# A decoder layer's last mixer projection, computed with seven block products in place of eight

## The chip, the core and the metric

The kernel runs on one core of one Trainium2 chip. A core has five engines that run side by side, each through its own list of instructions in order: PE multiplies matrices, DVE, ACT and POOL work on vectors, SP issues transfers. Engines wait for each other through semaphores. The metric is the time of one execution in microseconds (us) on the device, the median over the runs; lower is better. The profiler's trace is one execution of its own.

## The reference

One layer, 512 tokens of 1024 features, float32: a SwiGLU, a token mixer with two branches, a second SwiGLU, each added to the residual, and a final norm.

```python
x = x + 0.5 * swiglu(rms_norm(x, ffn1_norm), ffn1_w_gate, ffn1_w_up, ffn1_w_down)
x = x + token_mixer(rms_norm(x, mix_norm), w_in, ..., w_o)
x = x + 0.5 * swiglu(rms_norm(x, ffn2_norm), ffn2_w_gate, ffn2_w_up, ffn2_w_down)
return rms_norm(x, final_norm)
...
def swiglu(x, w_gate, w_up, w_down):
    return (jax.nn.silu(x @ w_gate) * (x @ w_up)) @ w_down
...
merged = jax.nn.sigmoid(g_a) * y_a + jax.nn.sigmoid(g_b) * y_b
return merged @ w_o                       # the end of token_mixer
```

The change is about the last line: `merged` is 512 x 1024, `w_o` is 1024 x 1024.

## The kernel before

**Matrix products.** Every float32 operand is split into a high part, rounded to the type that PE multiplies fast (fp32r), and the low rest; a product is three matmuls, high by high, high by low, low by high. A weight arrives by a transfer on SP's queue into `raw` (128 x 1024, 512 KB), ACT casts it to `whi`, DVE subtracts to `wlo`. There are four buffers of each of the three, and `stream` lists all pieces of weights in the order of their use; `weights()` (line 626) takes the next and has the following ones made.

**Stages.** First SwiGLU (`ffn_up_raw`, then `ffn_down`), the mixer's input projections and its recurrence (steps in the order of the table `MIXER`), the products of the two branches (the last is `ps_ob`, from line 1345), the output projection `rows` (771), the second SwiGLU (`ffn_up`, `ffn_down`).

**The output projection.** `m` holds eight tiles of `merged`, transposed: 128 features by 512 tokens. `rows` takes the eight pieces of `w_o`, and for each of four groups of 128 tokens and each half of 512 output features adds three matmuls of 512 columns to one of eight PSUM banks `ps_o`: 8 x 4 x 2 x 3 = 192 matmuls. The last three pieces (`TAIL`, 56) are run group by group, so that the groups end one after the other. Behind each group `mixed` (1373) adds the bank to the residual `x` (numbered tiles in the traces: one for each group and half), stores it to `x2d` and calls `renorm` (755): sums of squares on ACT (`sq`), root on ACT (after a load of its function table), reciprocal on DVE, scaled rows `xn` on DVE, four transposes on PE for each half into `ps_xt`, and from there on ACT and DVE the split operand `xh`, `xl` of the second SwiGLU, or the differences of tokens that it wants (`xt`, `t`, `tf1h` and so on, from `token_sums`, 813).

**Seven products for eight.** `ffn_up` and `ffn_down` cut both operands into 2 x 2 blocks and use the scheme that needs seven block products and some sums of blocks. The sums of the weights are made in DRAM, by transfers that copy and add (`transfer`, 519), issued on POOL's own DMA queue; the sums of the other operand (`form`) on DVE, split by `half_parts` (689): a cast on ACT and a subtraction on POOL, or for `VG` on whichever of DVE and POOL the planner takes. The products of `ffn_down` (922) go to pairs of banks `ps_dx`, `ps_dv`, `ps_dw`, in the order `DOWN_ORDER = (0, 2, 5, 4, 6, 3, 7)` (74), and `onto` adds each to the rows of the residual it belongs to. Product 3 ends token groups 0 and 1, product 7 groups 2 and 3, and `done` is called there. `ffn_up` starts with the products that read groups 0 and 1 alone (`UP_ORDER`, 72).

**Order.** `step_sums` (575) records the next transfer of the list `queue` at certain steps. All instructions are recorded first; `Plan.order` (251) then puts each engine's list in order, by program order among those whose operands are ready on its own estimate of durations. The engines follow these lists as they stand.

Of the kernel before, what the change touches and what calls it, by code (L numbers as in the profile page):

```python
# [55 lines left out]
TAIL = 3  # L56
# [393 lines left out]
def layer_kernel(ctx: ExitStack, tc: tile.TileContext, xT, x, vecs, cst, gu1, dn1, win, wout, wo, gu2, dn2, lora, gateup, gmix, gff2, gfin, out):  # L450
# [94 lines left out]
    def down_sums(name, w):  # L545
        got, groups = {}, []
        for j0 in range(0, FJ, 4):
            groups.append([])
            n = min(4, FJ - j0)
# [14 lines left out]
    def down_stream(w, downs):  # L564
        for b in DOWN_ORDER:
            for j in range(0, FJ, 2):
                n = min(2, FJ - j) * S
# [30 lines left out]
    for kt in range(KT):  # L598
        stream.append((wo[kt], D))
# [171 lines left out]
    def rows(hs, done):  # L771

        n = len(hs)
        accs = [[psum("ps_o") for _ in range(2)] for _ in range(NQ)]

        def one_row(ft, q, w, halves):
            hhi, hlo = hs[ft]
            whi, wlo = w
            for lh, r, k in ((hhi, whi, 0), (hhi, wlo, 1), (hlo, whi, 2)):
                for hf in halves:  # L780
                    T.matmul(accs[q][hf], lhsT=lh[:, sl(q)], rhs=r[:, hf * S:(hf + 1) * S],
                             start=ft == 0 and k == 0, stop=ft == n - 1 and k == 2)

        for ft in range(n - TAIL):
            w = weights()
            for q in range(NQ):
                one_row(ft, q, w, (0, 1))
            step_sums()
        tail = [weights(0) for ft in range(n - TAIL, n)]
        for q in range(NQ):  # L790
            for hf in range(2):
                for i in range(TAIL):
                    one_row(n - TAIL + i, q, tail[i], (hf,))
            done(q, accs[q])

# [126 lines left out]
    def ffn_down(hs, parts, res, done):  # L922

        banks = {n: [psum(n) for _ in range(2)] for n in ("ps_dx", "ps_dv", "ps_dw")}
# [23 lines left out]
        def onto(q, hf, ps, sign):  # L948
            x = res[q][hf]
            V.scalar_tensor_tensor(out=x, in0=ps, scalar=0.5 * sign, in1=x, op0=ALU.mult, op1=ALU.add)  # L950
# [3 lines left out]
        for b in DOWN_ORDER:  # L954
            ps = banks[{2: "ps_dv", 4: "ps_dw", 3: "ps_dw"}.get(b, "ps_dx")]
            x = forms.get(b) or [None] * FJ

            def one(j, w, rs):
# [387 lines left out]
    for dt in range(KT):  # L1346
# [63 lines left out]
def _layout(np, inp):  # L1410
# [27 lines left out]
    o["wo"] = w["w_o"].reshape(KT, P, D)  # L1438
# [32 lines left out]
```

## Time and profile before

| | us |
|---|---|
| median of the three runs | 1145.55 |
| lowest and highest of them | 1141.31, 1150.65 |
| the profiled execution | 1142.87 |
| its span, first to last instruction | 1141.1 |

In the profile a row of the timeline has the start (us from the span's start), the duration, engine, line, operation, tiles, shapes and count; in brackets stands the idle time of the engine ahead of it and what ended it. Nearly all rows have line 437, a helper that records every operation, so tiles tell the place. The table of stretches gives the busy time of each engine with the number of instructions in parentheses, the granted TensorE clock (1.00 is full), the share of the sixteen DMA engines' time and the rate.

### The profile page before, as it was taken

Reading aid. Unit: us, or ns where it says so; the run is one execution under the profiler, and the core shown is the slowest. Engines: PE = TensorE matmul, PEld = TensorE weight load, DVE = VectorE, ACT = ScalarE, POOL = GpSimd, SP = SyncE. Lnnn points to the kernel's source line nnn. Section 1 sums busy time; section 2 is a strip of 40 time slices with the busy share of each in tenths; the row PEclk is TensorE's granted clock in tenths of the full one; section 3 lists DMA queues with packets and bytes.
Section 4 is the critical chain, followed back from the end, with each engine's and each line's share of the span. In section 5 each row is a group of like instructions: output and inputs, shape, how many; then the busy total and the mean of one; then the engine's idle time right before and its main releaser. Section 6 shows DMA issues by size and latency. Waiting matters only on the chain.

```text
span 1141.1 us, 17088 instructions
## 1 busy us (share of the span) xinstructions
PE 1110.3 (97%) x6572; PEld 945.6 (83%) x6572; DVE 761.2 (67%) x1041; ACT 559.7 (49%) x964; POOL 305.3 (27%) x336
## 2 busy tenths in 40 slices
PE   8999999999999899989999999999999999999997
PEld 6888888888887777878777788888999999998886
DVE  5754454468867589995758742363987766768875
ACT  6422332236735776343655642333665555556744
POOL 4122121136840154234311121100011111217840
PEclk9999999999999989989999999999999999999999
DMA  8568686678899189889156679953576688875563
GB/s 307 171 221 222 239 219 197 177 189 278 282 296 362 43 193 280 232 237 256 53 139 180 154 226 330 306 179 116 174 221 248 213 216 271 229 246 185 190 190 119
DMA packets 67202, 244.87 MB, mean 215 GB/s; under 512 B 7089, under 2 KB 8113, under 8 KB 62129
## 3 DMA queue, kind: packets, MB, share of 16 engines
q1 hardware_dynamic: 48816, 151.51, 38.5%
q0 software_dynamic: 18304, 92.28, 32.4%
q8 instruction: 51, 0.84, 0.3%
q14 instruction: 31, 0.25, 0.1%
HBM read 237.47 MB, written 98.57 MB: 294 GB/s over the span
## 4 chain that ended last, share of the span: by engine, by line
PE 78%; DVE 8%; issue 6%; DMA 3%; ACT 2%; POOL 2%; SPq 0%; ACTq 0%; POOLq 0%; DVEq 0%
PE ps_gu L437 20%; PE ps_in L437 12%; PE ps_wx L437 11%; PE ps_dx L437 8%; PE ps_ww L437 5%; PE ps_o L437 4%; PE ps_dw L437 4%; PE ps_wc L437 3%; PE ps_dv L437 3%; PE ps_ob L437 2%; DVE wlo L437 2%; PE ps_oa L437 2%; DMA raw<-in_dn_dram 1%; DVE tmp L437 1%; PE ps_f L437 1%
## 5 line engine op out<-in xcount | busy, mean ns | idle before, releaser
L437 ACT CAST whi<-raw 128x1024 fp32r<-128x1024 f32 (+2 forms) x273 | 271.8, 997 | 441.8 <-issue 103.5
L437 DVE TENSOR_TENSOR wlo<-raw,whi 128x1024 fp32r<-128x1024 f32 (+2 forms) x273 | 333.6, 1228 | 184.1 <-ACT whi L437 178.5
L437 POOL TENSOR_TENSOR hp<-gg,hp 128x256 fp32r<-128x256 f32 x117 | 133.3, 1170 | 439.6 <-ACT hp L437 439.6
L437 PE MATMUL ps_gu<-xh,whi 128*128 128x512 f32 x352 | 137.1, 392 | 3.3 <-ACT whi L437 3.3
L437 PE MATMUL ps_in<-xl,whi 128*128 128x512 f32 (+1 forms) x360 | 137.5, 383 | 0.0
L437 PE MATMUL ps_in<-xh,wlo 128*128 128x512 f32 (+1 forms) x360 | 137.3, 382 | 0.0
L437 PE MATMUL ps_gu<-xl,whi 128*128 128x512 f32 x352 | 137.2, 391 | 0.0
L437 PE MATMUL ps_gu<-xh,wlo 128*128 128x512 f32 x352 | 137.2, 391 | 0.0
L437 PE MATMUL ps_in<-xh,whi 128*128 128x512 f32 (+1 forms) x360 | 137.0, 381 | 0.0
L437 PE MATMUL ps_dx<-whi,hp 128*128 128x512 f32 x352 | 112.8, 397 | 0.0
L437 PEld LDWEIGHTS ps_gu<-xh,whi 128*128 128x128 f32 x352 | 66.3, 188 | 18.6 <-ACT whi L437 4.6
L437 PEld LDWEIGHTS ps_dx<-whi,hp 128*128 128x128 f32 x352 | 66.6, 189 | 15.4
L437 PEld LDWEIGHTS ps_in<-xh,whi 128*128 128x128 f32 x360 | 68.2, 190 | 13.0 <-issue 0.4
L437 PEld LDWEIGHTS ps_in<-xl,whi 128*128 128x128 f32 x360 | 68.3, 190 | 12.6
L437 PEld LDWEIGHTS ps_in<-xh,wlo 128*128 128x128 f32 x360 | 68.2, 190 | 12.3
L437 PEld LDWEIGHTS ps_gu<-xh,wlo 128*128 128x128 f32 x352 | 66.6, 189 | 13.9
L437 PEld LDWEIGHTS ps_gu<-xl,whi 128*128 128x128 f32 x352 | 66.4, 189 | 13.8
L437 PE MATMUL ps_dx<-wlo,hp 128*128 128x512 f32 x176 | 69.8, 397 | 0.0
L437 DVE TENSOR_TENSOR uu<-ps_gu,rstd 128x512 f32<-128x512 f32 x22 | 15.2, 690 | 62.9 <-PE ps_gu L437 62.9
L437 PE MATMUL ps_dw<-whi,hp 128*128 128x512 f32 x176 | 55.6, 393 | 0.0
L437 ACT CAST hp<-gg 128x256 fp32r<-128x256 f32 x132 | 48.7, 404 | 13.1 <-DVE gg L437 13.0
L437 POOL DMA_DIRECT2D us<-in_gu_dram x36 | 30.7, 855 | 71.7 <-issue 60.4
(307 smaller groups left out, 2378.0 us busy)
## 6 DMA issues: line engine op xcount, KB each, us to landing
raw<-in_gu_dram SPq DMA_DIRECT2D x75, 512.0 KB, 4.1
us<-in_gu_dram POOLq DMA_DIRECT2D x30, 1024.0 KB, 9.5
raw<-us SPq DMA_DIRECT2D x44, 512.0 KB, 4.9
raw<-in_win_dram SPq DMA_DIRECT2D x42, 512.0 KB, 6.0
raw<-in_dn_dram SPq DMA_DIRECT2D x30, 512.0 KB, 4.7
d1s<-in_dn_dram POOLq DMA_DIRECT2D x12, 1024.0 KB, 8.3
ds<-in_dn_dram POOLq DMA_DIRECT2D x12, 1024.0 KB, 21.3
raw<-d1s SPq DMA_DIRECT2D x20, 512.0 KB, 6.4
```

What stands on the lines that cost most here:

```text
L437: return getattr(self.plan.engines[e], m)(**k)
```

## The change

The output projection goes through `ffn_down`, with four pairs of tiles of `m` where the SwiGLUs have eleven, and a scale of 1.0 where they have 0.5. `rows` and the split of `m` into `mhi`, `mlo` are gone. `w_o` is laid out in four blocks. `queue` gets eight more transfers, the sums of `w_o`'s blocks (`os`), behind those of the first SwiGLU; each step `pair` of the mixer now records four transfers and not two.

```diff
-    def down_sums(name, w):
+    def down_sums(name, w, nj=FJ):
...
-    def down_stream(w, downs):
+    def down_stream(w, downs, nj=FJ):
...
     downs1 = down_sums("d1s", dn1)
+    outs = down_sums("os", wo, KH)
     ups2 = up_sums("us", gu2)
...
-    for kt in range(KT):
-        stream.append((wo[kt], D))
+    down_stream(wo, outs, KH)
...
-    def rows(hs, done):
...
-    def ffn_down(hs, parts, res, done):
+    def ffn_down(hs, parts, res, done, scale=0.5):
+        nj = len(hs)
+        nt = 2 + nj % 2
...
             ends = b in (3, 7)
-            for j in range(FJ - TAIL if ends else FJ):
+            for j in range(nj - nt if ends else nj):
...
         if what == "pair":
-            step_sums(2)
+            step_sums(4)
...
-        hi = t2k("mhi", dt=F32R)
-        lo = t2k("mlo", dt=F32R)
-        A.copy(out=hi, in_=m_)
-        V.tensor_tensor(out=lo, in0=m_, in1=hi.bitcast(F32), op=ALU.subtract)
-        ms.append((hi, lo))
+        ms.append(m_)
...
-    def mixed(q, ps):
+    def mixed(q):
         for hf in range(2):
-            x2 = res[q][hf]
-            V.tensor_tensor(out=x2, in0=ps[hf], in1=x2, op=ALU.add)
-            Q.dma_start(out=x2d.keyed(2 * q + hf)[2 * q + hf], in_=x2)
+            Q.dma_start(out=x2d.keyed(2 * q + hf)[2 * q + hf], in_=res[q][hf])
         renorm("sb", q, res[q], gain, xg, take)
-    rows(ms, mixed)
+    ms = list(zip(ms[::2], ms[1::2]))
+    ffn_down(ms, [[half_parts(t, 0, VG) for t in two] for two in ms], res, mixed, 1.0)
```

One block product is 4 pairs x 2 groups of tokens x 3 = 24 matmuls of 512 columns, and takes two pieces of weights; seven are 168 matmuls and 14 pieces, six of them from `w_o` itself and eight from `os`.

Up to the last `ps_ob` PE's list is the same, row by row. On PE, at the end of the projection, there stood before (`ps_o` the projection, `ps_xt` the transposes; the end of the projection comes ten matmuls later, and `ps_wx`, the second SwiGLU's first product, follows it at once):

```order
L437 MATMUL ps_o<-whi,mhi 128x512
L437 MATMUL ps_o<-wlo,mhi 128x512
L437 MATMUL ps_xt<-cs,xn 128x128 x4
L437 MATMUL ps_o<-whi,mlo 128x512
L437 MATMUL ps_xt<-cs,xn 128x128 x4
L437 MATMUL ps_o<-whi,mhi 128x512
L437 MATMUL ps_o<-wlo,mhi 128x512
```

And now, at the same place (`ps_dx` is product 7, `ps_wx` and `ps_wc` are the second SwiGLU's first two products):

```order
L436 MATMUL ps_dx<-whi,hp 128x512 x2
L436 MATMUL ps_dx<-wlo,hp 128x512
L436 MATMUL ps_dx<-whi,hp 128x512
L436 MATMUL ps_xt<-cs,xn 128x128 x16
L436 MATMUL ps_wx<-xh,whi 128x256 x4
L436 MATMUL ps_wc<-xh,whi 128x256 x4
L436 MATMUL ps_wx<-xl,whi 128x256
```

The sixteen transposes of groups 0 and 1, which stood among the projection's matmuls, stand behind the last of them, and nothing else stands between.

On DVE the rows around the first `xn` were these (`x_5407` and `x_5429` are the two halves of group 0, `x_5432` and `x_5451` belong to groups 1 and 2, `sb` is the sum of squares and then the factor of the norm):

```order
L437 TENSOR_TENSOR x_5407<-ps_o,x_5407 128x512
L437 TENSOR_TENSOR x_5429<-ps_o,x_5429 128x512
L437 TENSOR_TENSOR sb_6757<-sb_6757 128x1
L437 TENSOR_TENSOR x_5432<-ps_o,x_5432 128x512
L437 RECIPROCAL sb_6757<-sb_6757 128x1
L437 SCALAR_TENSOR_TENSOR xn<-x_5407,sb_6757,gff_5339 128x512
L437 SCALAR_TENSOR_TENSOR xn<-x_5429,sb_6757,gff_5357 128x512
```

Now they are (`x_5429` and `x_5446` end groups 0 and 1 after product 3; `x_5451` and `x_5476` are those of groups 2 and 3 that wait for product 7, the first for its first half, the second for the last `ps_dx`):

```order
L436 SCALAR_TENSOR_TENSOR x_5429<-ps_dw,x_5429 128x512
L436 SCALAR_TENSOR_TENSOR x_5446<-ps_dw,x_5446 128x512
L436 TENSOR_TENSOR wlo<-raw,whi 128x1024
L436 TENSOR_TENSOR sb_6706<-sb_6706 128x1
L436 TENSOR_TENSOR sb_6715<-sb_6715 128x1
L436 SCALAR_TENSOR_TENSOR x_5451<-ps_dx,x_5451 128x512
L436 TENSOR_TENSOR wlo<-raw,whi 128x1024
L436 SCALAR_TENSOR_TENSOR x_5476<-ps_dx,x_5476 128x512
L436 RECIPROCAL sb_6706<-sb_6706 128x1
L436 RECIPROCAL sb_6715<-sb_6715 128x1
L436 TENSOR_TENSOR sb_6868<-sb_6868 128x1
L436 SCALAR_TENSOR_TENSOR xn<-x_5408,sb_6706,gff_5339 128x512
```

The first `xn`, for which the transposes wait, stands behind `x_5476`, which waits for the end of the projection, and behind a piece of weights.

On ACT the rows that `xn` waits for are now these (the casts of `whi` are pieces of the second SwiGLU's weights):

```order
L436 ACTIVATE sq,sb_6706<-x_5429 128x512
L436 ACTIVATE sq,sb_6715<-x_5446 128x512
L436 CAST whi<-raw 128x1024
L436 ACT_TABLE_LOAD
L436 ACTIVATE sb_6706<-sb_6706,eps_r 128x1
L436 ACTIVATE sb_6715<-sb_6715,eps_r 128x1
L436 ACTIVATE sq,sb_6868<-x_5451 128x512
L436 CAST whi<-raw 128x1024
L436 ACTIVATE sb_6868<-sb_6868,eps_r 128x1
L436 ACTIVATE sq,sb_6878<-x_5476 128x512
L436 COPY xt<-ps_xt 128x512
L436 CAST xh<-ps_xt 128x4x128
```

Before, the table was loaded between two sums of squares, with no cast of `whi` there; now one stands ahead of it and one behind the roots, ahead of the eight readers of `ps_xt`.

On POOL the list before had no vector work from the last branch product to the second SwiGLU. Its last transfers ahead of that were (`ds` are the sums of the last down projection's weights):

```order
L437 DMA ds_0_6179<-ds_0_6144 128x2048
L437 DMA ds_4_6350<-in_dn_dram 128x2048
L437 DMA ds_8_6736<-in_dn_dram 128x1536
L437 TENSOR_TENSOR hp<-gg,hp 128x256 x2
L437 DMA ds_4_6386<-ds_4_6350 128x2048
```

Now the low parts of `m` stand there, 19 of them on POOL and nine on DVE:

```order
L436 DMA ds_4_6394<-in_dn_dram 128x2048
L436 DMA us_8_5182<-us_8_5927 128x2x1024
L436 TENSOR_TENSOR hp<-m,hp 128x256 x7
L436 DMA ds_0_6151<-ds_0_6105 128x2048
L436 TENSOR_TENSOR hp<-m,hp 128x256
L436 DMA us_10_6002<-us_10_6092 64x2048
L436 TENSOR_TENSOR hp<-m,hp 128x256 x3
L436 DMA ds_4_6647<-in_dn_dram 128x2048
```

87 transfers stand ahead of the first of these `hp`, as many as stood ahead of the first `hp<-gg` of the second SwiGLU; six stand among them and four more behind the last, ahead of the second SwiGLU's `hp<-gg`.

More of the change, by code (lines that the diff above doesn't have):

```diff
@@ L54 @@
 DECAY_C = 0.6065306597126334
-TAIL = 3
 EARLY = 3
@@ L543, in up_sums @@
         return got
-    def down_sums(name, w):
+    def down_sums(name, w, nj=FJ):
         got, groups = {}, []
-        for j0 in range(0, FJ, 4):
+        for j0 in range(0, nj, 4):
             groups.append([])
-            n = min(4, FJ - j0)
+            n = min(4, nj - j0)
             js = slice(j0 * S, (j0 + n) * S)
@@ L562, in up_stream @@
             stream.append((w[j, b] if b < 4 else ups[b - 4, j], D))
-    def down_stream(w, downs):
+    def down_stream(w, downs, nj=FJ):
         for b in DOWN_ORDER:
-            for j in range(0, FJ, 2):
-                n = min(2, FJ - j) * S
+            for j in range(0, nj, 2):
+                n = min(2, nj - j) * S
                 stream.append((w[b, :, j * S:j * S + n] if b < 4 else downs[b - 4, j], n))
     downs1 = down_sums("d1s", dn1)
+    outs = down_sums("os", wo, KH)
     ups2 = up_sums("us", gu2)
@@ L769, in renorm @@
             V.tensor_tensor(out=lo, in0=ps, in1=hi.bitcast(F32), op=ALU.subtract)
-    def rows(hs, done):
[L773 to L794, printed above, removed]
     def halves(name, src):
@@ L949, in onto @@
             x = res[q][hf]
-            V.scalar_tensor_tensor(out=x, in0=ps, scalar=0.5 * sign, in1=x, op0=ALU.mult, op1=ALU.add)
+            V.scalar_tensor_tensor(out=x, in0=ps, scalar=scale * sign, in1=x, op0=ALU.mult, op1=ALU.add)
         adds = {0: [(0, 0, 1)], 2: [(0, 0, 1)], 5: [(0, 1, -1)], 4: [(2, 1, -1)], 6: [(2, 1, -1)], 3: [(0, 1, -1)], 7: [(2, 0, 1)]}
@@ L955, in ffn_down @@
             ps = banks[{2: "ps_dv", 4: "ps_dw", 3: "ps_dw"}.get(b, "ps_dx")]
-            x = forms.get(b) or [None] * FJ
+            x = forms.get(b) or [None] * nj
             def one(j, w, rs):
@@ L966, in one @@
                         T.matmul(ps[r], lhsT=lh[:, sl(r)], rhs=rh[:, js], start=b in (0, 2, 4) and j == 0 and k == 0,
-                                 stop=j == FJ - 1 and k == 2, skip_group_check=True)
+                                 stop=j == nj - 1 and k == 2, skip_group_check=True)
             ends = b in (3, 7)
-            for j in range(FJ - TAIL if ends else FJ):
+            for j in range(nj - nt if ends else nj):
                 if j % 2 == 0:
@@ L975, in ffn_down @@
             if ends:
-                tail = [weights() for _ in range(2)]
+                tail = [weights() for _ in range(0, nt, 2)]
                 for r in range(2):
-                    for j in range(FJ - TAIL, FJ):
-                        one(j, tail[(j - FJ + TAIL) // 2], [r])
+                    for j in range(nj - nt, nj):
+                        one(j, tail[(j - nj + nt) // 2], [r])
             for r in range(2):
@@ L1437, in _layout @@
     o["wout"] = wab.reshape(2, 4, P, 4, 2, P).transpose(0, 3, 2, 4, 1, 5).reshape(2, 4, P, D)
-    o["wo"] = w["w_o"].reshape(KT, P, D)
+    o["wo"] = w["w_o"].reshape(KH, 2, P, 2, S).transpose(1, 3, 2, 0, 4).reshape(4, P, KH * S)
     g2 = np.stack([w["ffn2_w_gate"], w["ffn2_w_up"]]).reshape(2, 2, KH, P, FJ, 2, P)
```

## The prediction

> **What bounds the kernel now.** I read the page's busy times first, then a table of stretches over the place of the change, then the timelines of PE, DVE, ACT and POOL there and at the one place where the code that is now used ran before, the end of the first SwiGLU.
>
> ```profile
> span 1141.1 us, 17088 instructions
> ...
> PE 1110.3 (97%) x6572; PEld 945.6 (83%) x6572; DVE 761.2 (67%) x1041; ACT 559.7 (49%) x964; POOL 305.3 (27%) x336
> ...
> q1 hardware_dynamic: 48816, 151.51, 38.5%
> q0 software_dynamic: 18304, 92.28, 32.4%
> ```
>
> PE is busy 97% of the span, so a matmul less is time gained wherever nothing else comes to stand in its place. The two queues' rows give prices of the sixteen DMA engines: 0.385 x 1141 / 151.51 = 2.9 us per MB for SP's loads, 1.5 us for a piece of weights, and 0.324 x 1141 / 92.28 = 4.0 us per MB for POOL's transfers, 4.2 us for one of 1024 KB.
>
> ```profile
> core 0: us, PE busy (x) PEld busy (x) DVE busy (x) ACT busy (x) POOL busy (x), PEclk, DMA share, GB/s
> 300.00:345.00 45.00, 45.00 (x195) 36.43 (x194) 31.16 (x39) 21.74 (x37) 26.58 (x38) 1.00 0.96 284
> 757.50:785.00 27.50, 27.50 (x120) 22.34 (x120) 8.30 (x9) 5.88 (x6) 0.00 (x0) 1.00 0.30 93
> 757.50:804.00 46.50, 46.50 (x212) 37.95 (x212) 20.08 (x31) 17.59 (x34) 0.00 (x0) 1.00 0.33 104
> 804.00:835.00 31.00, 29.85 (x251) 29.65 (x250) 30.76 (x50) 21.79 (x35) 0.00 (x0) 1.00 0.54 175
> ```
>
> The output projection is 757.5 to 804: PE without a gap, DVE 43%, POOL idle, DMA a third. Its first 27.5 us hold 120 matmuls and nothing else, 0.229 us each. From 804 the second SwiGLU begins; DVE is full there (30.76 of 31.00) and PE idle 1.15 us. The first stretch is the end of the first SwiGLU, the code that the projection now uses: PE full, DVE 69%, DMA 0.96.
>
> **What is removed.** 192 matmuls become 168: 24 x 0.229 = 5.5 us off PE's list, on the path. All else of the change is beside it or in its way.
>
> **What is added beside it.** Products take 168 x 0.229 = 38.5 us. DVE gets six pieces of `wlo` (1.23 each, 7.4), six more additions to the residual (14 for 8, 0.68 each, 4.1), 16 sums of blocks (0.41 each, 6.6) and nine `hp` for eight `mlo` (9 x 0.41 - 8 x 0.68 = -1.8): 20.1 + 16.3 = 36.4 us. Eight scalings and splits of groups 0 and 1 (some 0.68 each, 5.4) now stand behind the projection, which leaves 31 of 38.5.
>
> ```profile
> 327.33 0.68 DVE L437 SCALAR_TENSOR_TENSOR xr<-ps_dx,xr 128x512 f32<-128x512 f32 x1
> ...
> 786.58 1.23 DVE L437 TENSOR_TENSOR wlo<-raw,whi 128x1024 fp32r<-128x1024 f32 x1 [4.27 <-ACT whi L437]
> ...
> 760.24 0.68 DVE L437 TENSOR_TENSOR mlo<-m,mhi 128x512 fp32r<-128x512 f32 x1
> ...
> 815.14 0.41 DVE L437 TENSOR_TENSOR gg<-ps_wc,wq 128x256 f32<-128x256 f32 x1
> ...
> 759.22 0.62 ACT L437 CAST mhi<-m 128x512 fp32r<-128x512 f32 x1 [0.59 <-DVE m L437]
> ...
> L437 ACT CAST hp<-gg 128x256 fp32r<-128x256 f32 x132 | 48.7, 404 | 13.1 <-DVE gg L437 13.0
> ```
>
> That is 80%, against 69% under a full PE in 300 to 345; I take it as hidden, and its cover is the four buffers of `whi`: a piece lasts 12 x 0.229 = 2.7 us, so a cast that is released has 8 us until its piece is wanted. ACT gets six casts (1.05) and 28 half casts for eight (28 x 0.40 - 8 x 0.62): 17.6 + 12.5 = 30 us, hidden. On DMA, 14 pieces and the next SwiGLU's first (some 20 us), 5 MB of POOL's transfers (21) and stores (5) make 46 us in about 45: the third becomes full, as in 300 to 345. No cost while the buffers hold; at the projection's end it has one.
>
> **What the end costs.** Before, the renorm of groups 0 to 2 lay under the last pieces: transposes among matmuls, then `ps_wx` right behind `ps_o`.
>
> ```profile
> 799.87 0.60 PE L437 MATMUL ps_xt<-cs,xn 128*128 128x128 f32 x4
> 800.22 0.48 PE L437 MATMUL ps_o<-whi,mlo 128*128 128x512 f32 x1
> ...
> 803.53 0.40 PE L437 MATMUL ps_o<-whi,mlo 128*128 128x512 f32 x1
> 803.76 0.28 PE L437 MATMUL ps_wx<-xh,whi 128*128 128x256 f32 x1
> 803.88 0.28 PE L437 MATMUL ps_wx<-xl,whi 128*128 128x256 f32 x1
> ```
>
> Now all 16 transposes and `ps_wx` stand behind the last `ps_dx`, in order. Durations for that chain, from the same work before:
>
> ```profile
> 785.50 1.05 ACT L437 CAST whi<-raw 128x1024 fp32r<-128x1024 f32 x1 [4.44 <-PE ps_o L437]
> 788.45 0.63 ACT L437 ACTIVATE sq<-x 128x512 f32<-128x512 f32 x1 [1.89 <-DVE x L437]
> 788.98 0.18 ACT L437 ACTIVATION_READ_ACCUMULATOR sq<-x 128x1 f32 x1
> ...
> 791.14 1.28 ACT L437 ACT_TABLE_LOAD   x1
> 792.44 0.30 ACT L437 ACTIVATE sb<-sb,eps_r 128x1 f32<-128x1 f32 x1
> ...
> 794.99 0.59 ACT L437 COPY xt<-ps_xt 128x512 f32<-128x512 f32 x1 [1.64 <-PE ps_xt L437]
> 795.47 0.59 ACT L437 CAST xh<-ps_xt 128x512 fp32r<-128x512 f32 x1
> ```
>
> Let the last `ps_dx` leave PE at 0. In PE's list 19 matmuls stand behind the last `ps_dw`, so product 3 is out at -4.4, its result at -4.2. Two additions (0.68) end at -2.8, two sums of squares (0.71 with their read) at -2.1. ACT then casts a piece (1.05, to -1.05), loads the table (1.28, to 0.25), takes two roots (to 0.75) and a sum of squares (to 1.5). DVE adds product 7's last result (0.2 to 0.9), inverts, waits for that last sum until 1.5, adds, and makes the first `xn` by 2.4. So PE waits some 2.4 us for its first transposes. ACT goes on with a cast (to 2.55), a root (2.8), a sum of squares (3.5) and eight readers of `ps_xt`, 0.48 apart. `ps_wx` needs the sixth, done at 3.5 + 5 x 0.48 + 0.59 = 6.5; `ps_wc` the eighth, 7.45. In these 7.45 us PE does 16 transposes (four groups of 0.35, the step from 799.87 to 800.22) and four `ps_wx` of 0.12 (803.76 to 803.88), and is idle 5.6. The transposes cost the same before. So this term, +5.6, eats the 5.5.
>
> Three smaller terms. The same code's end in the first SwiGLU shows two of them:
>
> ```profile
> 345.47 0.40 PE L437 MATMUL ps_dx<-whi,hp 128*128 128x512 f32 x1
> 348.47 1.03 PE L437 MATMUL ps_xt<-cs,xn 128*128 128x128 f32 x4 [2.60 <-DVE xn L437]
> ...
> 344.77 1.05 ACT L437 CAST whi<-raw 128x1024 fp32r<-128x1024 f32 x1 [1.16 <-DMA raw<-d1s]
> 345.84 1.28 ACT L437 ACT_TABLE_LOAD   x1
> ...
> 345.00:348.50 3.50, 0.90 (x5) 0.41 (x3) 2.23 (x4) 3.47 (x6) 0.00 (x0) 1.00 1.01 365
> 348.50:352.00 3.50, 3.50 (x13) 3.03 (x14) 1.94 (x4) 1.72 (x3) 1.37 (x2) 0.52 1.03 408
> ...
> 396.00:399.80 3.80, 1.19 (x6) 0.65 (x4) 3.67 (x2) 3.80 (x8) 3.80 (x5) 1.00 0.39 46
> 399.80:403.20 3.40, 1.22 (x3) 1.02 (x4) 3.37 (x6) 3.38 (x4) 1.68 (x2) 0.50 1.06 210
> 403.20:406.60 3.40, 3.40 (x10) 2.63 (x9) 2.32 (x3) 0.46 (x2) 1.63 (x3) 0.50 0.57 159
> ```
>
> *Clock.* A stretch with PE nearly idle is followed by one of 3.4 us at half clock, two idle ones by two; a full PE loses 1.7 us in each. The 7.45 us make one or two: +1.7 to +3.4, I take 2.2, the lower with part of a second. The Trainium skill, "TensorE: Matmul & The Clock Gate", Part 1, has the half rate after at least one idle window of about 3.4 us; taken strictly, a window with transposes in it is not idle, and the sum would be 2.2 lower. Against it speaks that page's Part 4, by which transposes do not count as busy in the same way; the sum would be 1.2 higher. The window before 348.5 held 0.9 us of work and the clock fell, so the trace is nearer to Part 4; it changes no chance.
>
> *Late weights.* Two casts of pieces stand in ACT's chain, and one stood there at 344.77, 1.16 us late by its load under a full DMA. Bounds: 0, as loads at 785 had no wait, to +5, both late by twice that; I take the nearest row, +1.2.
>
> *Elsewhere.* The 1.15 us that PE idles behind 804 may go, as DVE catches up while PE waits: -1.1 to 0, I take -0.5. At 348.47 two of POOL's transfers come later than before, as the second sum of `os` must wait for the first; the late load may land earlier: -2.9 (1.2 and a stretch of half clock) to 0, I take -0.5. The other eight transfers' places in the mixer carry `us` for `us`, one group later, for free.
>
> Sum: -5.5 + 5.6 + 2.2 + 1.2 - 0.5 - 0.5 = +2.5. Against the profiled execution, 1142.87, that is 1145.4. This execution is 2.7 below the median, and the three runs spread over 9; I add nothing for that. From the ends of the bounds: -5.5 + 5.6 + 1.7 + 0 - 1.1 - 2.9 = -2.2, 1140.7; -5.5 + 5.6 + 3.4 + 5 = +8.5, 1151.4.
>
> **Rivals.** *The gain is kept (faster).* ACT and DVE would have to be ready as before 804, and only the sum of PE counts: 1142.87 - 5.5 - 1.1 = 1136.3, with the -2.9 at best 1133.4. For it: PE had no wait at 803.76. Against it: `x_5476` stands ahead of `xn` on DVE, so no speed of ACT brings the transposes under the matmuls.
>
> *POOL comes late (slower).* The low parts of `m`, wanted from PE's first `ps_dx`, stand behind 87 transfers on POOL. Before, the 87th was issued at 733.23, and waits there were for landings:
>
> ```profile
> 710.66 0.84 POOL L437 DMA_DIRECT2D ds<-ds  x1 [17.89 <-DMA ds<-in_dn_dram]
> ...
> 733.23 0.54 POOL L437 DMA_DIRECT2D ds<-in_dn_dram  x1 [4.16 <-issue]
> ...
> ds<-in_dn_dram POOLq DMA_DIRECT2D x5, 1024.0 KB, 23.3
> ...
> L437 POOL TENSOR_TENSOR hp<-gg,hp 128x256 fp32r<-128x256 f32 x117 | 133.3, 1170 | 439.6 <-ACT hp L437 439.6
> ```
>
> At 733 there are 24 us to spare. The 87th is now `us_8<-us_8`, which waits for a sum seven transfers ahead of it to land. With one landing of 23.3 us more it comes at 756, and with seven `hp` of 1.17 PE waits some 4; with a second, 27. It decides from about 750 on; price 12 to 25, time 1158 to 1170. Against it: the bytes ahead are about those of before (six of half size for four).
>
> *DVE becomes the bound.* If 31 of 38.5 us with its order cost a wait at each of four products, some 1.5 each, and weights come late too: +2.5 + 6 to 9, time 1151 to 1155. Against it: 45.00 of 45.00 in the first stretch.
>
> **How the numbers follow.** About 1% (11.5 us) is what a measurement of this kernel can tell from no change; 5.5 us is half of it. Chances: the forecast 0.63 (1140.7 to 1151.4), the gain kept 0.15 (1133 to 1140), DVE 0.10 (1151 to 1155), POOL 0.12 (1158 to 1170). The range 1137 to 1156 leaves out POOL and about a third of the gain kept: 0.17. Faster by over 1% (under 1134) is only the last part of the gain kept, 0.04; slower by over 1% is POOL, 0.12; within, 0.84.
>
> **What would show it.** Right: 168 matmuls `ps_dx`, `ps_dv`, `ps_dw` at 0.23 between `ps_ob` and `ps_wx`, without gaps; a wait of 2.4 to 5 us of the first `ps_xt` for `xn`, then one of some 2 of `ps_wx` for `xh`; a stretch at clock 0.5 behind it; `hp<-m` on POOL under way by 745. Wrong: `ps_wx` within 3 us of the last `ps_dx`; a gap at the first `ps_dx` released by POOL `hp`; or gaps among the products released by `wlo`. The sum fails if the clock stays at 1.00 or if loads land later than 10 us.

## The result: slower by 0.6%, where the forecast had 0.2%

| | kernel before | changed kernel | ratio, 95% interval |
|---|---|---|---|
| first runs, 7 of each | 1147.89 | 1153.53 (1151.53 to 1159.43) | 1.0065 [1.0043, 1.0088] |
| run again beside the experiments, 29 and 10 | 1146.18 | 1153.65 (1150.14 to 1159.05) | 1.0061 [1.0037, 1.0084] |
| forecast, against the profiled execution of before (1142.87) | | 1145.4 (+2.5) | 1.002 |

The loss is 5.6 us by the first pair of medians and 7.5 by the second: within 1%, inside the range of 1137 to 1156, but more than the +2.5 of the forecast; both intervals lie above 1. The ratios are estimated from the single runs, all of them but one of e18 (1158.04, 1.5% above the fastest of that kernel), and are not the quotients of the medians. The profiled execution of the changed kernel is the slowest of its seven (1159.43, span 1157.6), so lengths of stages are read beside those of a second profile of the same kernel (e11_after_again, 1151.03).

The table of stretches of the changed kernel over the projection, cut at the places where PE stops; the columns are those of the prediction:

```profile
core 0: us, PE busy (x) PEld busy (x) DVE busy (x) ACT busy (x) POOL busy (x), PEclk, DMA share, GB/s
767.30:785.00 17.70, 17.70 (x78) 14.36 (x77) 17.21 (x25) 10.69 (x20) 8.84 (x9) 1.00 0.97 283
785.00:793.80 8.80, 8.80 (x39) 6.82 (x37) 5.99 (x9) 2.11 (x2) 0.98 (x2) 1.00 1.04 243
793.80:799.60 5.80, 0.04 (x1) 0.00 (x0) 0.28 (x1) 1.35 (x3) 0.00 (x0) 0.78 0.97 339
799.60:803.60 4.00, 3.63 (x8) 2.43 (x9) 4.00 (x6) 2.24 (x5) 2.79 (x2) 0.50 0.59 187
...
814.70:817.30 2.60, 0.40 (x4) 0.34 (x4) 2.47 (x7) 2.59 (x8) 0.00 (x0) 1.00 1.00 224
817.30:820.90 3.60, 3.14 (x15) 2.50 (x13) 3.60 (x8) 3.52 (x9) 0.00 (x0) 0.53 1.03 231
```

Up to 793.8 it goes as forecast: PE without a gap, DMA full, DVE at 97% in the first stretch. Then there is a hole of 5.8 us that the kernel before does not have, with 4 us at half clock behind it (eight matmuls in 3.63 us, where full clock takes 1.8). The second pair of stretches, 814.7 to 820.9, is the end that the prediction worked out. PE's timeline at both places:

```profile
793.45 0.39 PE L436 MATMUL ps_dx<-whi,hp 128*128 128x512 f32 x1
799.65 0.80 PE L436 MATMUL ps_dx<-whi,hp 128*128 128x512 f32 x1 [5.81 <-ACT hp L436]
...
814.36 0.40 PE L436 MATMUL ps_dx<-whi,hp 128*128 128x512 f32 x1
816.96 3.48 PE L436 MATMUL ps_xt<-cs,xn 128*128 128x128 f32 x16 [2.20 <-DVE xn L436]
820.93 0.74 PE L436 MATMUL ps_wx<-xh,whi 128*128 128x256 f32 x4 [0.49 <-ACT xh L436]
821.91 0.74 PE L436 MATMUL ps_wc<-xh,whi 128*128 128x256 f32 x4 [0.24 <-ACT xh L436]
```

The hole lies six matmuls before the end of product 6 and is put down to a cast of `hp` on ACT. ACT's timeline at that time:

```profile
786.97 1.06 ACT L436 CAST whi<-raw 128x1024 fp32r<-128x1024 f32 x1 [0.29 <-PE ps_dw L436]
798.25 1.04 ACT L436 CAST whi<-raw 128x1024 fp32r<-128x1024 f32 x1 [10.22 <-DMA raw<-in_wo_dram]
799.20 0.40 ACT L436 CAST hp<-e 128x256 fp32r<-128x256 f32 x1
799.50 0.40 ACT L436 CAST hp<-m 128x256 fp32r<-128x256 f32 x1
```

And DVE's, which makes the low part of the same piece:

```profile
799.32 1.23 DVE L436 TENSOR_TENSOR wlo<-raw,whi 128x1024 fp32r<-128x1024 f32 x1 [8.18 <-ACT whi L436]
```

ACT idles 10.22 us for a piece of `w_o`, the second of product 3. The `hp` that PE needs for the last pair of product 6 stands behind it in ACT's list; its input has been ready since 790.8 on DVE. PE itself wants that piece only after those six matmuls and the twelve of product 3's first piece, 18 x 0.229 = 4.1 us after it stopped, at 798.0. It would have had `whi` at 799.3 (1.3 us late) and `wlo`, wanted one matmul later, at 800.55 (1.0 us more). So of 6.1 us of waits (5.81 and 0.32) some 2.3 are owed to the load as such, and the rest to the place of its cast ahead of `hp`. That division is an estimate worked out from the rows; no run changes this order alone. The loads in SP's timeline:

```profile
778.71 0.33 SPq L436 DMA_DIRECT2D raw<-in_wo_dram  x1
779.31 1.17 SPq L436 DMA_DIRECT2D x2d<-x  x2
781.04 0.49 SPq L436 DMA_DIRECT2D raw<-in_wo_dram  x1
783.75 4.54 SPq L436 DMA_DIRECT2D raw<-os  x2
789.31 14.28 SPq L436 DMA_DIRECT2D raw<-in_gu_dram  x3
```

The two of `in_wo` are product 3's pieces; the second was issued at 781.0, with 17 us to go until PE wants it. ACT's list came to it 7 us after the issue (788.0), and for `hp` to be ready when PE stopped (793.8) it had to land by 792.5, 11 us after the issue. The landings of the pieces of weights issued between 760 and 800 (least, median, most):

```profile
DMA to landing us min/median/max: 5.6/7.8/17.1
```

17.1 us is the one that ACT stood at (781.0 + 17.1 = 798.1). What filled the DMA engines is in POOL's timeline:

```profile
763.50 1.10 POOL L436 DMA_DIRECT2D us<-us  x1
765.63 2.96 POOL L436 TENSOR_TENSOR hp<-m,hp 128x256 fp32r<-128x256 f32 x2 [1.03 <-ACT hp L436]
771.69 1.47 POOL L436 TENSOR_TENSOR hp<-m,hp 128x256 fp32r<-128x256 f32 x1 [3.10 <-ACT hp L436]
773.11 0.56 POOL L436 DMA_DIRECT2D ds<-in_dn_dram  x1
...
778.06 1.22 POOL L436 TENSOR_TENSOR hp<-m,hp 128x256 fp32r<-128x256 f32 x1 [2.95 <-ACT hp L436]
779.23 0.81 POOL L436 DMA_DIRECT2D ds<-in_dn_dram  x1
...
785.14 0.84 POOL L436 DMA_DIRECT2D ds<-in_dn_dram  x1
```

The transfers stand among `hp<-m`, which keep step with the projection, so they are issued in it, these three 8 and 2 us ahead of the late load's issue and 4 us behind it. In the kernel before, nothing on POOL's list waits there, and all transfers recorded with the projection had been issued by 734, 23 us before it began.

The second loss is in the mixer's branch products. PE's and POOL's timelines in the stage of the pairs, 120 us earlier:

```profile
636.62 0.50 PE L436 MATMUL ps_sum<-hi,blk_r 128*128 128x512 f32 x1
...
641.48 0.50 PE L436 MATMUL ps_sum<-lo,blk_r 128*128 128x512 f32 x1 [3.02 <-POOL lo L436]
```

```profile
627.20 1.15 POOL L436 DMA_DIRECT2D us<-us  x1 [11.40 <-issue]
638.99 1.14 POOL L436 DMA_DIRECT2D us<-in_gu_dram  x1 [10.64 <-DVE xx L436]
639.71 1.71 POOL L436 TENSOR_TENSOR lo<-sq,hi 128x512 fp32r<-128x512 f32 x1
```

POOL's `lo`, for which PE waits, stands behind a transfer that adds onto a sum still on its way. The profile puts that transfer's wait down to DVE, but the one issued at 627.20 landed 11.5 us later, at 638.7, just ahead of the issue at 638.99. In the kernel before three transfers stand between the same two `lo` on POOL, and here four.

### The profile page after: what moved, and what is told of

Its sections match the earlier page's. It is cut to its first block, busy times and chain, and to the rows that moved or that the text cites. A ratio compares the mean times of both kernels' runs of the same rounds, so it can differ in the third digit from the quotient of the medians.

```text
span 1157.6 us, 17158 instructions
## 1 busy us (share of the span) xinstructions
PE 1113.4 (96%) x6548; PEld 945.6 (82%) x6548; DVE 781.5 (68%) x1070; ACT 570.5 (49%) x990; POOL 333.6 (29%) x363
## 4 chain that ended last, share of the span: by engine, by line
PE 79%; DVE 8%; issue 4%; ACT 4%; DMA 3%; POOL 1%; SPq 0%; DVEq 0%; ACTq 0%; POOLq 0%
PE ps_gu L436 20%; PE ps_in L436 12%; PE ps_wx L436 11%; PE ps_dx L436 10%; PE ps_ww L436 5%; PE ps_dw L436 4%; PE ps_dv L436 3%; PE ps_wc L436 3%; PE ps_ob L436 2%; DVE wlo L436 2%; PE ps_oa L436 2%; PE ps_f L436 1%; DVE tmp L436 1%; DMA raw<-in_dn_dram 1%; PE ps_s L436 1%
## 5 line engine op out<-in xcount | busy, mean ns | idle before, releaser
L436 ACT CAST whi<-raw 128x1024 fp32r<-128x1024 f32 (+2 forms) x279 | 277.7, 998 | 441.3 <-issue 103.0
L436 DVE TENSOR_TENSOR wlo<-raw,whi 128x1024 fp32r<-128x1024 f32 (+2 forms) x279 | 342.1, 1232 | 178.6 <-ACT whi L436 172.6
L436 PE MATMUL ps_dx<-whi,hp 128*128 128x512 f32 x416 | 134.6, 399 | 6.1 <-ACT hp L436 5.8
L436 PEld LDWEIGHTS ps_dx<-whi,hp 128*128 128x128 f32 x416 | 78.9, 190 | 25.4 <-ACT hp L436 6.2
L436 PE MATMUL ps_dx<-wlo,hp 128*128 128x512 f32 x208 | 82.8, 398 | 0.0
L436 PE MATMUL ps_dw<-whi,hp 128*128 128x512 f32 x208 | 66.4, 395 | 0.0
```

What stands on the lines that cost most here:

```text
L436: return getattr(self.plan.engines[e], m)(**k)
```

## The experiments

Lengths of stages, in us, each worked out from PE's timeline as the time from the first matmul of one tile to the first of the next. *First end*: `ps_dx` to `ps_in`. *Mixer*: `ps_in` to `ps_oa`. *Branches*: `ps_oa` to `ps_ob`. *Projection*: its first matmul to `ps_wx`. *Second*: `ps_wx` to the first `ps_dx` of the last down projection; where an expectation gives 200 to 206 us for the second SwiGLU's first part, it counts from its first `ps_ww`. The 22.3 us of `ps_ob`, the same in all, stand in no column. One execution each. *Moved* is what POOL's list has: transfers ahead of the projection's first `hp`, among them, behind (none of these `hp` exist where it is "-"). The ratio is against the kernel before on the same chip, whose medians there were 1145.4 to 1147.9.

| kernel | moved | first end | mixer | branches | projection | second | median | ratio, 95% |
|---|---|---|---|---|---|---|---|---|
| before | - | 113.3 | 223.5 | 148.0 | 46.2 | 223.4 | | 1 |
| after | 87, 6, 11 | 113.9 | 228.2 | 151.3 | 53.7 | 222.6 | 1153.53 | 1.0065 [1.0043, 1.0088] |
| e11_after_again | 87, 6, 11 | 114.4 | 222.5 | 150.7 | 52.9 | 222.5 | 1153.65 | 1.0061 [1.0037, 1.0084] |
| e1_sums_alone | - | 110.4 | 228.8 | 150.7 | 46.2 | 223.4 | 1147.24 | 1.0002 [0.9982, 1.0023] |
| e2_no_sums | 82, 4, 10 | 116.0 | 224.2 | 148.0 | 57.9 | 224.1 | 1158.08 | 1.0091 [1.0062, 1.0120] |
| e3_quiet | 87, 2, 15 | 111.4 | 223.9 | 152.3 | 45.1 | 228.8 | 1154.83 | 1.0065 [1.0039, 1.0090] |
| e4_order | 87, 6, 11 | 114.8 | 222.3 | 150.9 | 49.9 | 230.8 | 1159.37 | 1.0094 [1.0063, 1.0124] |
| e5_earlier | 92, 1, 11 | 116.3 | 225.6 | 148.1 | 43.3 | 224.4 | 1149.89 | 1.0026 [1.0005, 1.0047] |
| e6_earlier_order | 92, 1, 11 | 117.0 | 236.4 | 148.1 | 42.0 | 222.2 | 1147.52 | 1.0014 [0.9990, 1.0039] |
| e7_before_loaded | - | 116.4 | 223.2 | 148.0 | 46.2 | 223.4 | 1146.06 | 1.0001 [0.9982, 1.0021] |
| e8_earliest_order | 96, 1, 7 | 125.3 | 225.7 | 148.0 | 42.0 | 222.5 | 1155.31 | 1.0076 [1.0046, 1.0106] |
| e9_both_orders | 92, 1, 11 | 112.3 | 234.8 | 148.0 | 42.0 | 222.4 | 1152.95 | 1.0040 [1.0017, 1.0063] |
| e10_before_order | - | 110.4 | 231.3 | 153.6 | 46.3 | 223.8 | 1151.01 | 1.0016 [0.9991, 1.0041] |
| e12_gap_order | 90, 3, 11 | 118.2 | 224.1 | 158.6 | 41.6 | 222.7 | 1151.84 | 1.0043 [1.0023, 1.0062] |
| e13_before_earlier | - | 118.3 | 226.8 | 148.1 | 46.4 | 223.9 | 1153.98 | 1.0063 [1.0039, 1.0086] |
| e14_later4_order | 87, 2, 15 | 114.5 | 222.3 | 153.3 | 41.9 | 227.6 | 1148.12 | 1.0008 [0.9987, 1.0028] |
| e15_later3_order | 86, 0, 18 | 111.1 | 226.9 | 148.0 | 41.4 | 227.6 | 1143.20 | 0.9982 [0.9958, 1.0006] |
| e16_spread_order | 86, 0, 18 | 117.1 | 223.0 | 148.0 | 41.4 | 227.1 | 1143.74 | 0.9969 [0.9940, 0.9998] |
| e17_later3 | 86, 0, 18 | 113.8 | 228.3 | 148.0 | 43.2 | 226.1 | 1146.33 | 0.9984 [0.9962, 1.0007] |
| e18_spread_again | 86, 0, 18 | 113.0 | 228.5 | 148.0 | 41.4 | 228.2 | 1145.08 | 0.9975 [0.9954, 0.9996] |

How far a single execution can be trusted is in the table: before and e7 have the same code up to the branches, and differ by 3.1 us in the first end; after and e11 are one kernel, and differ by 5.7 in the mixer. The branches, the projection and the second part repeat within 1.1 us for the same code.

### What the mixer's eight transfers cost: e1_sums_alone

```diff
 # kernel before
-    def down_sums(name, w):
+    def down_sums(name, w, nj=FJ):
...
     downs1 = down_sums("d1s", dn1)
+    down_sums("os", dn1, KH)
...
         if what == "pair":
-            step_sums(2)
+            step_sums(4)
```

> The kernel before with eight more transfers of the kind of os in POOL's list (sums of blocks of the first down projection's weights, which nothing reads) and four transfers for two at each step pair; the output projection stays at eight products. Theory 1, the transfers cost in the mixer: the accumulating transfers that POOL waits for now stand ahead of its low parts, in the profile of after 3.0 us of PE's wait for lo near 612 with a stretch of half clock behind it: 1150 to 1153, 2 to 5 us above the kernel before. Rival, as the prediction had it, for free: within 1 us of the kernel before.

As a whole the rival, by the ratio. But its profile has theory 1's wait, 2.4 us for `lo`, and branches 2.7 us longer. They are 150.7 to 153.3 in all six profiles with four transfers at a step pair, and 148.0 or 148.1 in the others but two (e10 and e12, whose lists differ in the mixer too). The median does not show these 2.7 us. The profile's first end is shorter (110.4) and its mixer longer (228.8), and no experiment separates either from the scatter there; what makes up for the 2.7 us stays open. The run shows a second thing. Four of POOL's transfers were issued between 756.9 and 769.7, the projection began at 761.7, and the DMA engines were full:

```profile
757.00:765.00 8.00, 8.00 (x36) 6.47 (x36) 7.85 (x11) 3.12 (x5) 2.06 (x3) 1.00 1.04 315
765.00:785.00 20.00, 20.00 (x88) 16.23 (x87) 3.75 (x4) 4.01 (x4) 0.79 (x1) 1.00 1.02 279
```

The landings of the six pieces issued in 757 to 790, the last two of `w_o` and the first four of the second SwiGLU:

```profile
DMA to landing us min/median/max: 3.8/10.1/10.4
```

Loads of 10 us, and a projection of 46.2 as before. Full DMA engines are thus not enough for a loss; a landing of 17 us under eight products was not run. With eight products a piece lasts 24 matmuls, 5.5 us; with seven, 12 matmuls, 2.75 us. The same number of pieces ahead covers half the time, and six more loads and POOL's transfers run in it.

### Is it the sums of `w_o`? e2_no_sums

```diff
 # changed kernel; products 4 to 7 read blocks of w_o in place of sums
-    outs = down_sums("os", wo, KH)
-    down_stream(wo, outs, KH)
+    down_stream(wo, {(f, j): wo[f, :, j * S:(j + 2) * S] for f in range(4) for j in (0, 2)}, KH)
...
-            step_sums(4)
+            step_sums(2)
```

> The kernel after without the eight transfers os; products 4 to 7 of the projection read blocks of w_o in place of the sums, and each step pair records two transfers again. Theory 1, traffic (the os and the transfers that they push into the projection) is the loss: PE's wait of 5.8 us for hp behind a late load is gone and the mixer is as before, 1142 to 1147. Rival, the end of the projection (all transposes behind the last product) is the loss: 1150 to 1154, as after.

This kernel leaves the sums of `w_o`'s blocks out, so it tells of time alone. Theory 1 as I had put it fell: with POOL's 96 transfers of before and no `os` the projection is the longest of all (57.9), and the whole is above the rival's range too. Its timeline of ACT has the same wait:

```profile
791.22 1.04 ACT L436 CAST whi<-raw 128x1024 fp32r<-128x1024 f32 x1 [9.68 <-DMA raw<-in_wo_dram]
```

In POOL's timeline four transfers of `ds` are issued between 765.72 and 782.55, each behind an `hp`. With e3 below this says that what counts is where POOL's transfers run, not whose sums they are. The branches are as before (148.0), as expected.

### No transfers in the projection: e3_quiet

```diff
 # changed kernel: ffn_down has a number of steps, 0 for the projection
-            step_sums()
+            step_sums(steps)
...
 # ffn_up
-                step_sums()
+                step_sums(2 if j < 7 else 1)
```

> The kernel after, but no transfer of POOL's is recorded in the projection; the seven are recorded in the second SwiGLU's first part. Theory 1, the 512 KB load for product 3 lands 17 us after its issue because POOL's 1 MB transfers hold half of the DMA engines' time there, and ACT stands at it with hp behind: the wait of 5.8 us and the 3.4 us lost in 6.8 us of half clock behind it go, 1144 to 1149. Rival, the load is late by SP's own stream (14 pieces and the stores of x): within 2 us of the kernel after, 1151 to 1156.

In the place of the change theory 1 holds: no late piece (the longest landing in 755 to 800 is 8.0 us), no hole, 45.1 for 53.7. As a whole nothing is won: the second part takes 228.8, where PE waits 4.4 us in two pieces for `wq` on ACT, and the ratio is that of the changed kernel. The seven transfers were put two at a time into the next stage, and in the profiles it lost there 6.2 of the 8.6 us that the projection gained.

### Another order of products: e4_order

```diff
 # changed kernel, for the projection alone
-DOWN_ORDER = (0, 2, 5, 4, 6, 3, 7)
+DOWN_ORDER, EARLY_ORDER = (0, 2, 5, 4, 6, 3, 7), (0, 2, 5, 4, 3, 6, 7)
```

> The kernel after with product 3 of the projection ahead of product 6 (order 0, 2, 5, 4, 3, 6, 7), so that groups 0 and 1 end 48 matmuls (11 us) before the projection does; PE's list then has the sixteen transposes ahead of the last 29 matmuls of product 7. Theory 1, the chain at the end is the loss (2.2 us wait for xn, 3.5 us at half clock, then xh): it goes, 1146 to 1150. Rival, the late load is the loss and only comes at another product: within 2 us of the kernel after, 1151 to 1156.

Worse than either theory had it. The late load came at another product (ACT waits 9.61 us for `os`, PE 5.3 for `hp`), and the transposes, which now stand ahead of 29 matmuls, hold these up when the chain is late (7.2 us for `xn`). With the loads late, this order does not mend the end.

### The transfers elsewhere: e5, e6, e8, e12, e13

```diff
 # e5: with e3's step 0 in the projection
-                step_sums(2 if ft % 4 == 2 else 1)
+                step_sums(2 if ft % 2 == 0 or ft % 5 == 0 else 1)
...
-            step_sums(4)
+            step_sums(3)
 # e6: e5 and e4's order.  e8: step_sums(2) at every ft, 2 at pairs, and the order
 # e12: the order, step 0, 3 at pairs, and behind the first SwiGLU
+    step_sums(8)
 # e13: the kernel before with e5's first line
```

> The kernel after with POOL's transfers recorded earlier: 33 for 25 in the first part of the first SwiGLU, three for four at each step pair, none in the projection; one stands among the projection's hp in POOL's list in place of six, and eleven behind it. Theory 1, the late load is POOL's transfers in the projection: the projection takes 45 us as in e3_quiet (before 46.2, after 53.7), and nothing is bunched behind it: 1145 to 1149. Rival, the transfers cost wherever they stand, as the sixteen DMA engines are near full in all stages: PE waits for whi in the first SwiGLU or for operands in the second, 1150 to 1156.

> As e5_earlier, and product 3 of the projection ahead of product 6 as in e4_order, so that the transposes of groups 0 and 1 stand among the last matmuls of product 7. Theory 1, with loads on time the end's chain is hidden: the projection takes 40 to 42 us (168 matmuls are 38.5), 1140 to 1145. Rival, the order itself costs (the renorm then competes with product 6 and 7's operands and weights on ACT and DVE, as the 7.2 us wait for xn in e4_order may say): 1148 to 1156.

The projection comes out at 43.3 and at 42.0, so theory 1 holds for that stage in both, and with loads on time the order is worth 1.3 us there and 2.2 in the second part. The whole lies between the theories in both, 2.6 and 1.4 per mille above the kernel before.

> As e6_earlier_order, with two transfers at each step of the first SwiGLU's first part (40) and two at each step pair: one transfer of POOL's stands in the projection, seven behind it. Theory 1: 1139 to 1144, the mixer's waits for lo as before. Rival, the first SwiGLU's loads come late, as its DMA share rises by 15 x 4.0/250 = 0.24: 1148 to 1156.

> The kernel before, with the transfers of the first SwiGLU's first part recorded as in e5_earlier and e6_earlier_order (33 for 25), and nothing else changed; the same 96 transfers in all. Theory 1, e5 and e6 lose there what the projection gains: 1148 to 1150, 2 to 4 us above the kernel before, at the end of the first SwiGLU or in the mixer's first part. Rival, the place is free (within 1 us of before), and e5 and e6 lose by the number of transfers, not by where they stand.

> As e6_earlier_order, but with the transfers of the first SwiGLU at their old places; eight are recorded behind its end, where the DMA engines' share is 0.15 to 0.24 (375 to 400 us), three at each step pair, none in the projection (two stand among its hp in POOL's list). Theory 1, the transfers cost only where the DMA engines are full: 1141 to 1145, with the projection at 42 us. Rival, they cost at any place, since a stage filled with them delays the mixer's loads or POOL's low parts: 1147 to 1152.

e13 points to where the gain went: the kernel before, with nothing but its own transfers moved into the first SwiGLU, loses 6.3 per mille, more than theory 1 gave it. Its first end, 118.3, is 2 to 5 above those of before and e7. e8, with more of them there, has 125.3. e12, with eight recorded at the gap of the DMA engines behind the first SwiGLU, has the projection at 41.6, but branches 10 us longer; its lists are others in the mixer, and I did not follow that up. The rivals won in e8 and e12.

### A test that missed: e7_before_loaded

```diff
 # kernel before, in rows, behind each of the first five pieces
             step_sums()
+            at = len(plan.ops) - 1
+            transfer(Part(Slot(dram, [P, 4 * S], F32, "dram", f"ex{ft}")), dn1[0, :, 0:4 * S], 0)().deps.add(at)
```

> The kernel before with five more transfers of 1 MB, which nothing reads, recorded behind the first five pieces of its projection, so that some seven of POOL's transfers run beside its eight pieces. Theory 1, only a full set of DMA engines makes loads late: 0.33 + 7 x 4.0/46 is a share of 0.94, and the loads there have slack: within 2 us of the kernel before. Rival, any 1 MB transfer of POOL's beside SP's loads makes one late by 10 us: 1150 to 1158.

The time is the one that theory 1 gave, but not for its reason. POOL's timeline:

```profile
751.38 0.52 POOL L437 DMA_DIRECT2D ex<-in_dn_dram  x1 [2.56 <-issue]
843.01 0.92 POOL L437 TENSOR_TENSOR hp<-gg,hp 128x256 fp32r<-128x256 f32 x1 [91.11 <-ACT hp L437]
```

The last of the five was issued some 8 us before the projection began (760.0). Their bytes still moved at its start: the DMA engines' share was 1.03 in 760 to 765 and 0.49 in 765 to 785. So the run loads the projection for its first part alone. The place at which a transfer is recorded sets its place in the list only; where nothing ahead of it waits, it runs ahead. In the changed kernel it is the waiting work among them, `hp<-m`, that holds them back into the stage. e1 is the run that answers the question.

### The order in the first SwiGLU: e9_both_orders, e10_before_order

```diff
 # e9: e6 and, as e10 alone in the kernel before:
-    down_stream(dn1, downs1)
+    down_stream(dn1, downs1, order=EARLY_ORDER)
...
-    ffn_down(hs, parts, res, first_done)
+    ffn_down(hs, parts, res, first_done, order=EARLY_ORDER)
```

> As e6_earlier_order, and the same order of products (3 ahead of 6) in the down projection of the first SwiGLU, whose end has the same chain: PE waits 2.6 to 4.2 us for xn there and loses some 1.7 to 3.4 us in half clock behind it, in every kernel so far. Theory 1, both ends are chains that only the order hides: the first SwiGLU's end is 3 to 6 us shorter than in e6_earlier_order (110 to 114 us from its first ps_dx to the first ps_in, where e5 and e6 took 116 and 117): 1140 to 1145, below the kernel before. Rival, a late load under the full DMA engines there stops ACT all the same, as in e4_order: 1147 to 1152.

> The kernel before, its projection with eight products, and only the order of products in the first SwiGLU's down projection changed as in e9_both_orders. It separates what e9 has from the seven products and what from the first SwiGLU's order. Theory 1: 3 to 5 us below the kernel before, 1140 to 1143, and e9 stands 2 to 4 us lower still. Rival: the order brings nothing where the DMA engines are full (within 2 us of before), and what e9 gains is the projection's.

The first end is shorter (112.3 for e6's 117.0; 110.4 for 113.3 before, though e1 has 110.4 with the old order). The mixer's first part, from `ps_in` to `ps_lora`, is longer by as much or more (25.7 us for e6's 21.3; 24.9 for 18.1 before), as PE waits 4.2 there for `xn`. Neither is faster, and I did not follow this up.

### The changed kernel again: e11_after_again

> The kernel after, unchanged, beside the others on this chip. Theory 1, its loss is the late load in the projection and the mixer's wait for lo, in all of its runs: 1151 to 1156, a projection of 52 to 55 us with PE's wait for hp of 5 to 7 us, and 150 to 152 us of the branch products ahead of it (before 148). Rival, the profiled execution was an odd one: the projection under 50 us here, with the time lost at other places.

PE's timeline, at the two places of the first profile:

```profile
791.25 0.80 PE L436 MATMUL ps_dx<-whi,hp 128*128 128x512 f32 x1 [4.93 <-ACT hp L436]
...
808.76 3.39 PE L436 MATMUL ps_xt<-cs,xn 128*128 128x128 f32 x16 [2.21 <-DVE xn L436]
```

Theory 1 holds, with the hole, the wait for `lo` (2.5) and the end as in the first profile. Only its bound for `hp`, 5 to 7, was missed by 0.1.

### The transfers behind the projection, one by one: e14 to e18

```diff
 # e4's order and e3's step 0; in ffn_up, e14 (4 at pairs) and e15 (3 at pairs):
-                step_sums()
+                step_sums(2 if j % 4 == 2 else 1)     # e14
+                step_sums(2 if j % 3 else 1)          # e15, and e17 without the order
 # e16: as e15, the second at product 4 of the row
+            if b == 4 and j % 3:
+                step_sums()
```

> As after with product 3 ahead of 6 in the projection and no transfer recorded in it; the three that are missing are recorded with rows 2, 6 and 10 of the second SwiGLU's first part (fourteen stand behind the projection in POOL's list, one for every two of hp). Theory 1: the projection takes 42 us, the mixer's branch products 150 to 152 as in after, the second SwiGLU's first part 200 to 203: 1143 to 1148. Rival, fourteen transfers there cost 4 to 6 us however they are spread, as in e3_quiet: 1149 to 1154.

> As e14_later4_order, but three transfers for four at each step pair, and seven rows of the second SwiGLU's first part with two; no transfer stands in the projection and eighteen behind it. Theory 1: the branch products take 148 us again and the projection 42: 1141 to 1146, not slower than the kernel before. Rival, eighteen transfers behind the projection make the second SwiGLU's loads late or its sums late for the last down projection: 1149 to 1156.

> As e15_later3_order, the second transfer of a row of the second SwiGLU's first part recorded at its product 4 and not together with the first, some 10 us apart. Theory 1, two transfers at once make the load late that ACT stands at (3.0 us wait for wq and half clock behind it): the stage takes 201 to 203 us for 205.8, 1139 to 1143. Rival, eighteen transfers are too many for the stage wherever they stand: within 1.5 us of e15_later3_order, 1142 to 1145.

> As e15_later3_order with the products of the projection in the old order (3 behind 6), so that the transposes stand behind the last product again. Theory, the chain of the prediction without a late load (2.4 us wait for xn, then xh, half clock): the projection takes 43 to 46 us for 41.4, 1145 to 1148. Rival, the end is hidden by the quiet queue alone: within 1 us of e15_later3_order, 1142 to 1145.

> The kernel of e16_spread_order once more. If the projection's 4.8 us less the second SwiGLU's 3.7 us more and what the first SwiGLU gets by later transfers is a gain in all runs: a ratio of 0.995 to 0.999, interval below 1. Rival, chance of one set of runs: 0.999 to 1.002.

e14 and e15 differ at the branches: 153.3 with `lo` late by 3.4 us, and 148.0 without. In e15 pieces land in time in the projection (755 to 800):

```profile
DMA to landing us min/median/max: 3.5/4.1/5.4
```

The projection is 41.4, and the whole 1.8 per mille under the kernel before, not yet beyond its interval. The second part still has one wait of the same kind, as PE's waits in 925 to 945 say:

```profile
PE ps_wx L436 <- ACT wq L436: 3.0, 1, 3.0
```

e16 was to remove it and did not: POOL's transfers stand behind `hp<-gg` there, were again issued in pairs, and the wait is 2.3. Its rival was right on that stage, within 0.5 us of e15. Its ratio is 0.9969, and 0.9975 when measured again, both intervals below 1: this kernel, with seven products and POOL's transfers kept out of the projection, is faster than the kernel before by some 0.3%. How much of that the products bring is not shown. The projection is 4.8 us shorter and the second part 3.7 and 4.8 longer, and no run has eight products with the transfers recorded as here. e17 prices the order with loads on time: 43.2 for 41.4 in the projection and 0.7 more in the first products behind it. The whole does not show these 2.5 us: the ratios of e15 and e17 are 0.9982 and 0.9984, as the rival had it.

## Why the prediction was off, by its own steps

- **-5.5 for 24 matmuls**: right. Without late loads and with the transposes among the products the projection is 41.4 (46.2 before), that is 38.5 of products, 1.4 of transposes and 1.5 of the rest.
- **+5.6 for the end's chain**: right in the changed kernel. The first `xn` came 2.20 late (2.4 in the prediction) and `ps_wc` began 7.3 us behind the last `ps_dx` (814.6 to 821.91; 7.45). With loads on time the same order cost less, 2.5 us in e17 against e15 and 3.5 in e5 against e6.
- **+2.2 for half clock at the end**: wrong, counted twice. The stretch came where it was forecast (0.53 in 817.3 to 820.9), but in it PE was waiting for ACT in any case: ACT, whose readers of `ps_xt` set its pace, was busy 3.52 of 3.60 us there, so the chain's 7.45 us hold the slower transposes (3.48 us for 1.4). The window before 348.5 held matmuls alone, as the first transpose starts at 348.47; other than the prediction has it, it says nothing of how transposes count for the clock.
- **+1.2 for late weights, bounds 0 to +5**: this step failed. It measured some 8 us: 5.81 and 0.32 of waits and 1.8 of half clock. I took the lateness from one row of 1.16 us, at the end alone, though I had the DMA engines as full and a row quoted under the rivals had 23.3 us from issue to landing (of POOL's transfers). I reckoned the cover from a cast to PE's need of its own piece (8 us), and not to the need of what stands behind that cast on ACT. And "no cost while the buffers hold" took POOL's transfers as spread over the stage, without a look at which of them its list would now hold back into it. Of my list of what would break the sum, "loads land later than 10 us" is what came.
- **The other eight transfers' places in the mixer, for free**: failed, by 2.7 to 3.3 us of the branches (e1 shows the wait, but no loss in the whole). Four transfers for three ahead of `lo` put it behind a landing that came too late for PE. I had compared the transfers and not what stands behind them.
- **-0.5 behind 804**: right, 222.6 and 222.5 for 223.4 in the second part. **-0.5 at the first SwiGLU's end**: not to be told; 113.9 and 114.4 lie between 113.3 and 116.4 of the old list.
- **The rivals**: POOL was not late with its first `hp`, and DVE not the bound, though its nine `hp` took 0.81 us each where the sum has 0.41. "The gain is kept" was turned down for a right reason, the place of `xn`, and e6 and e15 show that a change of order lifts that reason.

With the failed terms at their measured size the sum is -5.5 + 5.6 + 8 + 3 - 1 = +10; the stages of the first profile say +7.5 + 3.3 - 0.8 = +10 and those of the second +6.7 + 2.7 - 0.9 = +8.5, beside +5.6 and +7.5 in the medians. They leave out the mixer, 4.7 us longer in the first profile and 1.0 shorter in the second. What stays open: how the hole divides between the load and ACT's order, and the scatter in the first end and the mixer, from run to run and from list to list, which also moved e6, e9, e10 and e12.

## What to carry to other kernels

When products get shorter per byte of weights, compare the landing time of a load under full DMA engines with the time that the pieces ahead of it cover: here a piece went from 5.5 to 2.75 us, and PE felt a landing of 17. Transfers that share a list with waiting vector work run when that work does; look where the list lets them go, not where they were recorded. And a load that an engine waits for holds up all that stands behind it in that engine's list, so a late weight stops a product that doesn't use it.

## What the hardware showed

In the stretch 767 to 800 the two queues had about equal shares of the DMA engines' time (the queue's number, packets, MB, share):

```profile
q0 software_dynamic: 581, 4.10, 52.9%
q1 hardware_dynamic: 1551, 5.14, 45.1%
```

A 512 KB load took up to 17.1 us to land beside POOL's 1 MB transfers. With none of them issued in the stage, the loads of e15 took 5.4 at most, and those of the kernel before in 757 to 800 took 3.4 to 4.2. The Trainium skill, "DMA: Bandwidth & Descriptors", section "Queues, rings and completion order", says that each engine takes packets in turn from the queues that have some. The trace does not show this: the shares of time are near equal, but the packets that it counts are 581 against 1551, and no run here changed their size.

A stretch as long as the one at half clock, in which PE was busy for 1.30 of 3.50 us, transposes included, was still followed by half clock (table of stretches of the changed kernel):

```profile
813.80:817.30 3.50, 1.30 (x8) 0.77 (x7) 3.37 (x8) 3.49 (x8) 0.00 (x0) 1.00 1.02 225
817.30:820.70 3.40, 3.14 (x15) 2.50 (x13) 3.40 (x8) 3.31 (x8) 0.00 (x0) 0.53 1.05 236
```

The Trainium skill, "TensorE: Matmul & The Clock Gate", Part 1, asks for an idle window; here a third of a window busy was idle enough.

In five of the twenty profiles (the first of the changed kernel, e1, e6, e17, e18) PE stands 2.0 to 3.0 us at one place in the mixer, put down to "issue", with half clock behind it. In the first:

```profile
517.24 0.32 PE L436 MATMUL ps_i<-un,noff 128*32 128x32 f32 x4 [2.46 <-issue]
```

Four of these mixers took 228.2 to 228.8 us and e6's 236.4; of the others all but e9 and e10 took 222.3 to 226.9. Kernels of both kinds have it, and what PE stands at there the profile does not show.
